# Streaming encoder step on one core: twelve conditioning pieces in the gating stage, and two pauses in each pair of columns of the column sums

## The chip, the core and the metric

The kernel runs on one core of a Trainium2 chip. The metric is the device time of one execution in microseconds. Before the change it is 2128.83 us, the median of three runs (2127.75 to 2129.07).

## What is computed

The reference is one step of a small encoder of two layers with d = 1024, for a prompt of 1024 rows and a sample of 32 rows, which share all weights but have conditioning vectors of their own:

```
mod = silu(c) @ w_ada[i] + b_ada[i]                 # 6 x 1024 per layer: sh1, sc1, gt1, sh2, sc2, gt2
h   = rmsnorm(x) * (1 + sc1) + sh1
mix = layer 0: gating mixer:  u, v = split(gelu(h @ w_in)); v = rmsnorm(v)
               mix = (u * (W_s v + b_s)) @ w_out    # W_s within chunks of 128 rows, 8 groups
      layer 1: pooling mixer: trailing means over 2, 4, 8, 16 rows, minus h, a matrix per group
x   = x + gt1 * rmsnorm(mix)
h   = rmsnorm(x) * (1 + sc2) + sh2
x   = x + gt2 * rmsnorm(relu(h @ w_up)^2 @ w_down)  # 1024 -> 4096 -> 1024
```

All arrays are float32. `w_ada` alone holds 2 x 1024 x 6144 numbers, which are used once, for two vectors.

## The kernel before, in words

**Tiles.** The 1056 rows are the columns of three tiles (`TILES`): tile 0 and tile 1 of 384 prompt columns, tile 2 of 256 prompt and 32 sample columns. Channels lie along the partitions. Every large product is made of three matmuls of float32r (high x high, high x low, low x high, `products` L952 to L963), so each weight is split into a high part (ScalarE, L441) and a low part (VectorE, by `tt`, whose line in the profile is L80).

**Stages.** (1) Run-in with a hand-written order. (2) The `v` half of the gating mixer's first product (`pv`). (3) The gating stage, from about 245 to 617 us: six entries of `mixes` (L372), each two groups and a list of tiles. Mixes 0 and 1 take all three tiles, mixes 2 and 3 tile 0 alone, mixes 4 and 5 tiles 1 and 2. `sgu_item` makes for each tile four `up` blocks (`pu`, 24 matmuls each), after each second one the gating product (`psp`) with `gate`, and leaves `down` (`po`, eight output blocks of twelve matmuls) pending: it is emitted after the first `up` block of the next tile (`flush`, L1534). (4) Layer 0's feed-forward network: `passes` of 512 hidden channels. Some passes take one tile; the six passes `COMBINED[0]` take tiles 0 and 1 together in a form with seven products in place of eight (`combined_item`, `pf_0a` to `pf_1c`, L1625), from about 756 to 1147 us. These need, beside the columns themselves, four sums and differences of columns of tiles 0 and 1, which `sums_of_columns` (L1808) makes ahead of the stage: `sum_columns` (L1839) once for each of four pairs of columns. (5) Tile 2's passes, woven with the pooling mixer; layer 1's passes; four paired passes (`COMBINED[1]`) from about 1655 to 1908 us; tile 2's last passes and the output.

**The weight stream.** All weights come through one list, `stream`, in the order in which they are used: gating weights by `w_groups`, feed-forward weights by `w_chunk`, and between them the conditioning pieces of `w_ada`, 512 KB each, by `some_ada` (L347), which appends the next n of the list `rest`. Loads are issued on SP's queue by `issue` (L409) into three buffers `raw` (L178) in the order of the stream. `stream_step` (L658) takes the next item: `do_w` splits a weight, `do_s` (L463) makes the seven weight combinations of a paired pass out of a load, and `do_ada` (L539) multiplies a conditioning piece by the conditioning values: four VectorE operations of 128 x 512 per piece into `aa`, and after every fourth piece two transposes, a reduction and, later, a small matmul (`ada`, L528).

**The order.** The source is a program that plans as it emits. `time["pe"]` and `time["dve"]` (L66) add up estimated times of TensorE and VectorE; `tick` keeps VectorE's at most 4 us behind. After each block `weave` (L758) takes at most one item of the stream (not a conditioning piece while VectorE's clock is more than 0.5 us ahead of TensorE's, `stream_waits` L695), then pulls `fillers` while VectorE's clock is behind. `need_w` (L704), called where a matmul needs a weight, takes items until that weight is there, whatever they are. A gating weight may be split when the weight eight places ahead of it has been used for the last time (L651). Fillers are generators: norms, residuals, the pooling mixer, the column sums. What a generator yields tells `pull` (L728) how to go on: `False` leaves it in its place, `True` puts it on `sticky`, so that it is the next to be pulled, and a number closes it until the planner's TensorE clock has passed the present by as many microseconds, while the next filler may go. `finish` pulls a filler to its end at once where its result is needed.

The instructions thus emitted are then put in an order for each engine by the framework, which schedules by readiness with the emission order as rank; on the chip each engine runs its list in that fixed order.

**Where the change touches.** In the loop over `mixes` (L374 to L377), in the loop over `passes` (L378 to L381), and in `sum_columns` (two `yield True`, L1855 and L1869). There, for each pair of columns, three loads from `md` are followed by four subtractions on VectorE, four roundings on ScalarE (L1866, L1868) and four low parts on VectorE.

Of the kernel before, what the change touches and what calls it, by code (L numbers as in the profile page):

```python
# [35 lines left out]
def tile_stream_encoder_step(  # L36
# [128 lines left out]
    def t_m(name):  # L165
        return work.tile([P, 384], F32, tag="m", bufs=3, name=name)
# [99 lines left out]
    def w_groups(n):  # L266
        gs, _ = mixes[n]
        for g in gs:
            for k in range(2):
                f = 2 * g + k  # L270
                add_w(
                    ("u", n, g, k),
                    sgu_w_in[0][:, f * P : (f + 1) * P].rearrange("(k p) f -> p k f", p=P),
                    (8, P),
                )
        for q in range(2):
            for g in gs:
                add_w(
                    ("o", n, g, q),
                    sgu_w_out[0][g * 256 : (g + 1) * 256, q * 512 : (q + 1) * 512].rearrange(  # L280
                        "(k p) d -> p k d", p=P
                    ),
                    (2, 512),
                )

    def w_chunk(n):
        l, c, _ = passes[n]
        if n in combined:
            for i in range(2):
                f0 = c * 512 + i * 256  # L290
                for q in range(2):
                    stream.append(
                        (
                            "s",
                            ("up", n, i, q),
                            ffn_w_up[l][q * 512 : (q + 1) * 512, f0 : f0 + 256].rearrange(
                                "(k p) f -> p k f", p=P
                            ),
                            (4, 256),
                        )  # L300
                    )
        for j in range(0 if n in combined else 4):
            f = 4 * c + j
            add_w(
                ("up", n, j),
                ffn_w_up[l][:, f * P : (f + 1) * P].rearrange("(k p) f -> p k f", p=P),
                (8, P),
            )
        for q in range(4):
            add_w(  # L310
                ("dn", n, q),
                ffn_w_down[l][c * 512 : (c + 1) * 512, q * 256 : (q + 1) * 256].rearrange(
                    "(j p) d -> p j d", p=P
                ),
                (4, 256),
            )
# [26 lines left out]
    combined = [n for r in runs for n in r]  # L343
# [3 lines left out]
    def some_ada(n):  # L347
        for _ in range(min(n, len(rest))):
            add, l, j = rest.pop(0)
            add(l, j)  # L350
# [22 lines left out]
    mixes += [((4, 5), every[1:]), ((6, 7), every[1:])]  # L373
    for n in range(len(mixes)):  # L374
        w_groups(n)
        if n < 2:
            some_ada(8)  # L377
    for n, (l, c, tiles) in enumerate(passes):  # L378
        w_chunk(n)
        if n in combined:  # L380
            some_ada(2 if l else 6 if n + 1 in combined else 2)  # L381
    assert not rest

    worder = [s[1] for s in stream if s[0] in "ws"]
# [70 lines left out]
    def temp(i):  # L455
        return scratch[:, 1024 + 384 * i : 1408 + 384 * i]
# [1351 lines left out]
    def sums_of_columns(l):  # L1808
        begun.add(l)
        n = ncol[0]  # L1810
        rooms = [room(part, NT - 1, f"sums_{part}", F32R) for part in "hl"]
        pieces = [
            r.rearrange("p k n -> p (k n)")[:, i * n : (i + 1) * n] for r in rooms for i in range(6)
        ]
        for name, tag, bufs, shape, k in (
            ("c", "c", 3, [P, 384], 1),
            ("r", "rr", 2, [P, 384], 1),
            ("w", "W", W_SLOTS, [P, 1024], 2),
        ):
            for i in range(w_taken[l] if tag == "W" else bufs):  # L1820
                x = work.tile(shape, F32R, tag=tag, bufs=bufs, name=f"sums_{name}{i}")
                pieces += [x[:, m * n : (m + 1) * n] for m in range(k)]
        for i in range(3):
            x = small.tile([P, 2, n], F32R, tag="x3", bufs=3, name=f"sums_x{i}")
            pieces += [x[:, 0], x[:, 1]]
        wide = late.tile([P, 2, 256], F32R, tag="wg", bufs=1, name="sums_g")
        pieces.append(wide.rearrange("p a b -> p (a b)")[:, :n])
        sums["spare"] = [pieces.pop(17) for _ in range(6)]
        sums["his"] = [pieces.pop(0) for _ in range(8)]
        sums["los"] = pieces  # L1830
        sums["parts"] = {}
        dsh = small.tile([P, 4], F32, tag="st", bufs=6, name="dshift")
        sh = shift[:, l, 1, :, 0].rearrange("p (k a) -> p k a", a=2)
        tt(out=dsh, in0=sh[:, :, 1], in1=sh[:, :, 0], op=ALU.subtract)
        sums["dsh"] = dsh
        for i in range(4):
            yield from sum_columns(l, i, (hh[0][:, 2 * i, :], hl[0][:, 2 * i, :]))

    def sum_columns(l, i, homes):  # L1839
        n = ncol[0]  # L1840
        dsh = sums["dsh"]
        home = {0: homes[0], 2: homes[1]}
        t1, t3, t2 = (temp(m) for m in range(3))
        t4 = t_m(f"sums_m{i}")
        nc.sync.dma_start(t1, md[1][:, 2 * i, :])
        nc.sync.dma_start(
            scratch[:, 1408:2176].rearrange("p (a n) -> p a n", a=2), md[0][:, 2 * i : 2 * i + 2, :]
        )
        nc.sync.dma_start(t4, md[1][:, 2 * i + 1, :])
        yield 3.0  # L1850
        tt(out=t1, in0=t3, in1=t1, op=ALU.subtract)
        tt(out=t3, in0=t2, in1=t3, op=ALU.subtract)
        tt(out=t2, in0=t2, in1=t1, op=ALU.subtract)
        tt(out=t4, in0=t4, in1=t2, op=ALU.subtract)
        yield True  # L1855
        todo = (
            (2, t3, dsh[:, i : i + 1]),
            (0, t1, None),
            (1, t2, shift[:, l, 1, 2 * i + 1, 0:1]),
            (3, t4, None),  # L1860
        )
        for j, src, b in todo:
            hi, lo = home[j] if j in home else sums["his"].pop(0), sums["los"].pop()
            sums["parts"][j, i] = hi, lo
            if b is None:
                act(out=hi, in_=src, func=AF.Copy)  # L1866
            else:
                act(out=hi, in_=src, func=AF.Identity, bias=b, scale=1.0)  # L1868
        yield True  # L1869
        for j, src, b in todo:  # L1870
            hi, lo = sums["parts"][j, i]
            if b is None:
                tt(out=lo, in0=src, in1=hi.bitcast(F32), op=ALU.subtract)
            else:
                stt(
                    out=lo,
                    in0=src,
                    scalar=b,
                    in1=hi.bitcast(F32),
                    op0=ALU.add,  # L1880
                    op1=ALU.subtract,
                )
        yield False
# [338 lines left out]
```

## Time and profile before

| | |
|---|---|
| median of the runs | 2128.83 us |
| profiled execution: its time, its span | 2128.48 us, 2126.7 us |
| VectorE busy, ScalarE busy | 74%, 49% of the span |
| DMA | 326.08 MB, 153 GB/s on average |
| VectorE busy in the gating stage (245 to 617 us) | 242.4 of 372 us |
| VectorE busy in the first paired stage (754 to 1147 us) | 317.6 of 393 us |
| VectorE busy in the second paired stage (1650 to 1908 us) | 165.5 of 258 us |
| conditioning pieces: loads, median time to landing | 96 of 512 KB, 4.6 us |

A span runs from the first to the last instruction. Busy times are unions of the instructions' times; matmuls overlap, so that one of 384 columns is listed with some 0.33 us while a new one begins about every 0.17 us. PE is TensorE, DVE VectorE, ACT ScalarE, SP the queue that issues the loads. In a line of the waits stand the waiting group, what released it, the time in all, the count and the longest. In a line of a timeline stand the start, the duration, engine, line, operation, out<-in, shape and count, and in brackets the idle time before it with its releaser. In a line of windows stand the stretch, its length, the busy time of PE, PEld, DVE, ACT and POOL, the granted clock of TensorE, the busy share of the DMA engines and GB/s. A line of the chain has start, duration and what ran, with the count.

### The profile page before, as it was taken

The numbers are of one execution on the slowest core, as the hardware profiler recorded it, in microseconds if no ns is written. First come the engines' busy times: TensorE is split into PE (matmuls) and PEld (weight loads), VectorE is DVE, ScalarE is ACT, GpSimd is POOL, SyncE is SP. The second block draws the span as 40 slices with busy tenths as digits, with TensorE's granted clock in tenths as the row PEclk, the third lists the DMA queues.
The fourth block names the chain that finished last, engine by engine and source line by source line (L and its number), as shares of the span: only waits on it lengthen the run. The fifth ranks groups of instructions, "written<-read, shape, count | busy, mean of one in ns | idle before, by whom it ended". The sixth has DMA issues, their size and how long they took to land.

```text
span 2126.7 us, 33204 instructions
## 1 busy us (share of the span) xinstructions
PE 2109.9 (99%) x12993; PEld 2035.4 (96%) x12993; DVE 1564.9 (74%) x2854; ACT 1032.6 (49%) x1808; POOL 15.3 (1%) x34
## 2 busy tenths in 40 slices
PE   9999999999999999999999999999999999999998
PEld 6878999999999999999999999999999999999998
DVE  6687747566879659987877987967768575588664
ACT  5534322234447554344446666665455453366454
POOL 0000000000000000000000000000000000000100
PEclk9999999999999999999999999999999999999999
DMA  8487524353537614343345675565356232258861
GB/s 309 140 278 211 168 85 131 93 150 104 174 94 241 190 52 148 121 137 111 116 156 175 197 246 164 154 197 166 108 155 194 70 106 78 62 172 254 205 184 38
DMA packets 368178, 326.08 MB, mean 153 GB/s; under 512 B 39858, under 2 KB 330202, under 8 KB 368020
## 3 DMA queue, kind: packets, MB, share of 16 engines
q1 hardware_dynamic: 367348, 323.06, 49.8%
q8 instruction: 102, 1.67, 0.3%
q0 software_dynamic: 640, 0.88, 0.1%
q14 instruction: 56, 0.46, 0.1%
q10 hardware_dynamic: 32, 0.01, 0.0%
HBM read 283.41 MB, written 40.49 MB: 152 GB/s over the span
## 4 chain that ended last, share of the span: by engine, by line
PE 88%; DVE 5%; DMA 4%; ACT 2%; issue 1%; SPq 0%; DVEq 0%; ACTq 0%
PE pg L961 10%; PE pg L963 10%; PE pg L962 10%; PE pf L961 6%; PE pf L962 5%; PE pf L963 5%; PE pf_0a L1625 4%; PE po L962 3%; PE po L961 3%; PE po L963 3%; PE pu L961 3%; PE pu L963 3%; PE pu L962 3%; PE pv L988 2%; PE pv L990 2%; PE pv L989 2%
## 5 line engine op out<-in xcount | busy, mean ns | idle before, releaser
L961 PE MATMUL pg<-fh,wh_dn 128*128 128x384 f32 (+1 forms) x1296 | 415.4, 321 | 2.7 <-ACT fh L1374 2.2
L963 PE MATMUL pg<-fh,wl_dn 128*128 128x384 f32 (+1 forms) x1296 | 412.2, 318 | 0.0
L962 PE MATMUL pg<-fl,wh_dn 128*128 128x384 f32 (+1 forms) x1296 | 412.1, 318 | 0.0
L961 PE MATMUL pf<-hh,wh_up 128*128 128x288 f32 (+1 forms) x896 | 281.0, 314 | 0.0
L962 PE MATMUL pf<-hl,wh_up 128*128 128x288 f32 (+1 forms) x896 | 279.2, 312 | 0.1
L963 PE MATMUL pf<-hh,wl_up 128*128 128x288 f32 (+1 forms) x896 | 278.8, 311 | 0.0
L961 PEld LDWEIGHTS pg<-fh,wh_dn 128*128 128x128 f32 x1296 | 243.1, 188 | 5.9 <-ACT fh L1374 3.6
L962 PEld LDWEIGHTS pg<-fl,wh_dn 128*128 128x128 f32 x1296 | 243.2, 188 | 0.7
L963 PEld LDWEIGHTS pg<-fh,wl_dn 128*128 128x128 f32 x1296 | 243.2, 188 | 0.7 <-DVE wl_dn L80 0.7
L80 DVE TENSOR_TENSOR acc<-acc,pg 128x384 f32<-128x384 f32 (+1 forms) x336 | 171.7, 515 | 64.6 <-PE pg L963 63.0
L80 DVE SCALAR_TENSOR_TENSOR aa<-raw,csil,aa 128x512 f32<-128x512 f32 (+1 forms) x364 | 204.9, 619 | 13.2 <-DMA raw<-in_w_ada_dram 13.2
L80 DVE TENSOR_TENSOR wl_dn<-raw,wh_dn 128x1024 fp32r<-128x1024 f32 x118 | 143.4, 1219 | 42.0 <-ACT wh_dn L441 41.0
L962 PEld LDWEIGHTS pf<-hl,wh_up 128*128 128x128 f32 x896 | 168.2, 188 | 0.9 <-DVE hl L80 0.3
L961 PEld LDWEIGHTS pf<-hh,wh_up 128*128 128x128 f32 x896 | 168.0, 188 | 0.9 <-ACT r L1549 0.2
L963 PEld LDWEIGHTS pf<-hh,wl_up 128*128 128x128 f32 x896 | 168.4, 188 | 0.0
L80 DVE TENSOR_TENSOR wl_up<-raw,wh_up 128x1024 fp32r<-128x1024 f32 (+2 forms) x141 | 128.2, 917 | 46.2 <-ACT wh_up L441 38.6
L441 ACT ACTIVATE wh_dn<-raw 128x1024 fp32r<-128x1024 f32 x118 | 124.1, 1055 | 75.3 <-PE pg L962 61.0
L441 ACT ACTIVATE wh_up<-raw 128x1024 fp32r<-128x1024 f32 x81 | 85.8, 1059 | 90.0 <-PE pf L962 56.9
L961 PE MATMUL pu<-hh,wh_u 128*128 128x384 f32 (+1 forms) x384 | 125.8, 328 | 0.0
L961 PE MATMUL po<-ush,wh_o 128*128 128x384 f32 (+1 forms) x384 | 123.5, 322 | 0.0
L963 PE MATMUL pu<-hh,wl_u 128*128 128x384 f32 (+1 forms) x384 | 123.4, 321 | 0.0
L962 PE MATMUL pu<-hl,wh_u 128*128 128x384 f32 (+1 forms) x384 | 123.4, 321 | 0.0
(456 smaller groups left out, 4556.0 us busy)
## 6 DMA issues: line engine op xcount, KB each, us to landing
raw<-in_ffn_w_up_dram SPq DMA_DIRECT2D x121, 512.0 KB, 4.1
raw<-in_ffn_w_down_dram SPq DMA_DIRECT2D x118, 512.0 KB, 3.5
raw<-in_w_ada_dram SPq DMA_DIRECT2D x96, 512.0 KB, 4.6
raw<-in_sgu_w_in_dram SPq DMA_DIRECT2D x40, 512.0 KB, 4.1
raws<-in_ffn_w_down_dram SPq DMA_DIRECT2D x30, 512.0 KB, 4.3
raws<-in_ffn_w_up_dram SPq DMA_DIRECT2D x27, 512.0 KB, 4.7
xd<-acc SPq DMA_DIRECT2D x8, 1536.0 KB, 7.4
raw<-in_sgu_w_out_dram SPq DMA_DIRECT2D x24, 512.0 KB, 3.7
```

The lines of the kernel that those rows point to most:

```text
L80: return op(out, *args, **kw)
L441: act(out=wh, in_=r, func=AF.Copy)
L961: mm(ps[:, :n], wh, rh, start=begin and i == 0, stop=False)
L962: mm(ps[:, :n], wh, rl, start=False, stop=False)
L963: mm(ps[:, :n], wl, rh, start=False, stop=end and i == last)
L988: mm(ps[:m, :], a_h, wh[:, o : o + 512], start=k == 0, stop=False)
L989: mm(ps[:m, :], a_h, wl[:, o : o + 512], start=False, stop=False)
L990: mm(ps[:m, :], a_l, wh[:, o : o + 512], start=False, stop=k == KB - 1)
L1625: mm(ps[:, :n], u, v, start=first and k == 0 and x == 0, stop=k == 3 and x == 2, skip_group_check=True,)
```

## The change

First, where conditioning pieces stand in the stream. Before, eight follow the gating weights of each of mixes 0 and 1; in the paired passes of layer 0 six follow each pass and two the last one, in those of layer 1 two each. After, eight, eight, eight and four follow mixes 0 to 3, five each (three for the last) the paired passes of layer 0, and none those of layer 1. So twelve more stand in the gating stage, four fewer in the first paired stage and eight fewer in the second; the order of the pieces among themselves is the same.

Second, `sum_columns` yields 1.5 in place of `True` after its subtractions and again after its roundings.

```
     for n in range(len(mixes)):
         w_groups(n)
-        if n < 2:
-            some_ada(8)
+        some_ada((8, 8, 8, 4, 0, 0)[n])
     for n, (l, c, tiles) in enumerate(passes):
         w_chunk(n)
         if n in combined:
-            some_ada(2 if l else 6 if n + 1 in combined else 2)
+            some_ada(0 if l else 5 if n + 1 in combined else 3)
...
         tt(out=t4, in0=t4, in1=t2, op=ALU.subtract)
-        yield True
+        yield 1.5
         todo = (
...
                 act(out=hi, in_=src, func=AF.Identity, bias=b, scale=1.0)
-        yield True
+        yield 1.5
         for j, src, b in todo:
```

More of the change, by code (lines that the diff above doesn't have):

```diff
@@ L375, in tile_stream_encoder_step @@
         w_groups(n)
-        if n < 2:
-            some_ada(8)
+        some_ada((8, 8, 8, 4, 0, 0)[n])
     for n, (l, c, tiles) in enumerate(passes):
@@ L1854, in sum_columns @@
         tt(out=t4, in0=t4, in1=t2, op=ALU.subtract)
-        yield True
+        yield 1.5
         todo = (
@@ L1868, in sum_columns @@
                 act(out=hi, in_=src, func=AF.Identity, bias=b, scale=1.0)
-        yield True
+        yield 1.5
         for j, src, b in todo:
```

2 lines of the change are left out of this document (1 added, 1 removed).

## The prediction

> **What bounds the kernel now.** I read the page first, then the waits of TensorE by stage, the table of windows, and last the timelines of VectorE, ScalarE and the DMA queue around the places that the change touches.
>
> ```profile
> PE 2109.9 (99%) x12993; PEld 2035.4 (96%) x12993; DVE 1564.9 (74%) x2854; ACT 1032.6 (49%) x1808; POOL 15.3 (1%) x34
> ```
>
> TensorE is the bound: 16.8 of 2126.7 us are idle. A change that leaves the matmuls alone can win only such idle time, and loses whatever new wait it gives TensorE. The waits, in the order gating stage (245 to 660 us), first paired feed-forward stage with the building of its sums (660 to 1130), second one (1560 to 1910):
>
> ```profile
> PE psp L1467 <- DMA vl<-vd: 0.7, 1, 0.7
> ```
> ```profile
> PE pg L961 <- ACT fh L1374: 1.4, 1, 1.4
> PE pf_1c L1625 <- DVE acc L80: 0.6, 1, 0.6
> PE pf_1a L1625 <- ACT acc L1642: 0.6, 1, 0.6
> ```
> ```profile
> PE pg L962 <- DVE sums_w L80: 1.5, 2, 0.8
> PE pg L961 <- ACT fh L1374: 0.8, 1, 0.8
> PE pf_1a L1625 <- ACT acc L1642: 0.6, 1, 0.6
> PE pg L961 <- DVE acc L80: 0.4, 1, 0.4
> PE pf_1c L1625 <- DVE acc L80: 0.2, 1, 0.2
> ```
>
> The stage that receives twelve pieces has no wait on VectorE today; the two that give them up have 6.1 us of waits together. A matmul of 384 columns shows 0.33 us but starts every 0.174 us (2.10 us for twelve, row below), so each wait also costs about 0.16 us of lost overlap: the nine of the last two fences are some 7.5 us in all, the most that could be won.
>
> **Gating stage: what comes in.** The weight stream is taken in order. `weave` (L758) takes at most one piece a call, eight calls per tile; an item of the stream that a matmul needs now makes `need_w` (L704) take all that stand before it at once. After the change eight conditioning pieces stand behind the weights of mix 2 and four behind those of mix 3. Mixes 2 and 3 have one tile each, 36 us. Of mix 2's eight calls two find nothing ready and four go to its own `o` weights (which follow those of mix 1 as these are released), so that two pieces are taken after its last two `up` blocks. The other six are forced by the first `up` of mix 3, which needs the `u` weight behind them, and they then rank ahead of that weight and of the accumulations of mix 2's `down`, emitted later (`flush`, L1534).
>
> When that weight is needed and when it is ready today:
>
> ```profile
> 447.99 0.42 PE L961 MATMUL pu<-hh,wh_u 128*128 128x384 f32 x1
> ```
> ```profile
> 433.36 1.22 DVE L80 TENSOR_TENSOR wl_o<-raw,wh_o 128x1024 fp32r<-128x1024 f32 x1
> 434.49 1.22 DVE L80 TENSOR_TENSOR wl_u<-raw,wh_u 128x1024 fp32r<-128x1024 f32 x1
> 437.82 0.62 DVE L80 SCALAR_TENSOR_TENSOR s<-psp,vec,bs 128x384 f32<-128x384 f32 x1 [2.11 <-PE psp L1467]
> ...
> 443.28 0.68 DVE L80 TENSOR_SCALAR wr<-wt,rv 128x128 f32<-128x128 f32 x3
> ...
> 447.60 0.62 DVE L80 SCALAR_TENSOR_TENSOR s<-psp,vec,bs 128x384 f32<-128x384 f32 x1 [2.51 <-PE psp L1467]
> ```
> ```profile
> 428.28 7.83 SPq L431 DMA_DIRECT2D raw<-in_sgu_w_in_dram  x4
> ```
>
> It is split at 434.5 to 435.7 and needed at 448.0: 12.3 us to spare. The four loads that start at 428.28 would be conditioning pieces. What such a piece costs, and how eight of them went in mix 1 of this kernel:
>
> ```profile
> 328.66 9.20 SPq L431 DMA_DIRECT2D raw<-in_w_ada_dram  x4
> ...
> 344.44 3.91 SPq L431 DMA_DIRECT2D raw<-in_w_ada_dram  x2
> ...
> 357.35 2.56 SPq L431 DMA_DIRECT2D raw<-in_w_ada_dram  x2
> ```
> ```profile
> 359.89 2.06 DVE L80 SCALAR_TENSOR_TENSOR aa<-raw,csil,aa 128x512 f32<-128x512 f32 x3
> ...
> 369.70 0.54 DVE L80 TENSOR_TENSOR acc<-acc,po 128x384 f32<-128x384 f32 x1
> 370.16 1.30 DVE L568 STREAM_TRANSPOSE raw<-aa 128x512 f32<-128x512 f32 x2
> 371.50 1.22 DVE L571 TENSOR_REDUCE sums<-raw 128x32 f32<-128x1024 f32 x1
> ```
>
> Three operations take 2.06 us, so a piece of four takes 2.7; every fourth piece adds transposes and a reduction, 2.5. Eight: 8 x 2.7 + 2 x 2.5 = 26.6 us of VectorE, with three raw buffers. By row the whole set of eight took from 328.7 to 372.7 in mix 1, 44 us, where nobody waited.
>
> The sum of VectorE's work. The first piece lands some 4 us after 428.3, at 432.3; until 448.0 that is 15.7 us. Ahead of the pieces stand one `wl_o` (1.2), the gating work from 437.82 to 443.96 less the `wl_u` in it (6.1 - 1.2 = 4.9), and the start of the second gating (0.6): 6.7. So 9.0 of 26.6 us are done by 448.0 and 17.6 remain; with the rest of the second gating (4.3, as in the first) and the weight itself (1.2) it is ready 23 us late, at 471. TensorE has cover: matmuls are put in an order other than the source's when operands are late (the next fence shows three products interleaved), so it can begin mix 2's `down`. There twelve matmuls take 2.1 us per output block, and three PSUM buffers (`ps_dn`, L159) hold three blocks, 6.3 us; the accumulations that free them rank behind the forced pieces. Two thirds of the first `up` block needs only `wh_u`, which needs no VectorE: another 2.8 us.
>
> ```profile
> 832.73 0.33 PE L1625 MATMUL pf_0b<-hl,wh_up 128*128 128x384 f32 x1
> 832.90 0.34 PE L1625 MATMUL pf_0c<-hl,sh_up 128*128 128x384 f32 x1
> 833.08 0.54 PE L1625 MATMUL pf_0a<-hh,wh_up 128*128 128x384 f32 x2
> ```
> ```profile
> 770.80 2.10 PE pf_0a L1625 x12
> ```
>
> That leaves 23 - 9.1 = 14 us of standstill. The other end: accumulations slip in between the pieces as at 369.70, all eight blocks (16.7 us) cover, and their 8 x 0.54 = 4.3 us are added: 23 + 4.3 - 16.7 - 2.8 = 8 us. The 44-us row gives, from 428.3, 472.3 plus 1.2 for the weight against 448.0 + 16.7: 8.8. I take **+9.5 us**, near that row, since those pieces had the same loads and gating work around them; 6 to 16 as bounds. The four pieces in mix 3 (10.8 + 2.5 = 13.3 us) are forced in the same way by mix 4's first `up`, but only four stand there, and 36 us hold them with the eight weights (9.8) and the gating work (11): 0, and up to 2 if not. On SP's queue a piece's load that waits for a raw buffer holds the `vl` loads of the next gating; the one such wait in the trace is 0.7 us, so 0, at most 1. The bytes (12 x 512 KB) are little in a stage that moves 123 GB/s. Fillers (tile 0's residual) are pulled only while the planner's VectorE clock is behind TensorE's, and by its rates (0.16 + 512/840 us an operation) twelve pieces add 12 x 3.1 us and more to it, so they start up to 40 us later; VectorE is busy 242 of 372 us of the stage, so they still end before the first feed-forward product needs them; 0, at most 2.
>
> ```profile
> 245.00:617.00 372.00, 371.26 (x2410) 369.93 (x2408) 242.40 (x473) 118.82 (x194) 2.50 (x8) 1.00 0.41 123
> ...
> 1908.00:2127.00 219.00, 211.30 (x1592) 210.68 (x1590) 145.61 (x218) 113.94 (x195) 9.95 (x16) 0.98 0.61 169
> ```
> ```profile
> 1.36 5.49 PE warm L1042 x12
> ...
> 41.37 16.77 PE pv L1203 x73
> ```
>
> A standstill of this length may also cost clock. The granted clock is 1.00 throughout and falls only in the last stage, where TensorE ends early; waits of up to 1.4 us lose nothing. After the start's idle time twelve matmuls of 512 columns took 5.49 us, against 12 x 0.23 = 2.8 later: 2.7 us lost. Between 0 and 2.7 I take **+1.5**. The Trainium skill ("TensorE: Matmul & The Clock Gate", Part 1, "What's actually happening") says that the clock halves after an idle window of about 3.4 us and comes back after a busy one. By it one to two windows at half rate would cost an estimated 1.7 to 3.4 us, and the sum would be 2135.7 to 2137.4; no run here shows such a gap yet.
>
> **What the paired stages give up.** In the second one all eight pieces go. Two rows before its waits at 1809 to 1815:
>
> ```profile
> 1805.32 2.73 DVE L80 SCALAR_TENSOR_TENSOR aa<-raw,csil,aa 128x512 f32<-128x512 f32 x4
> 1808.88 0.42 DVE L80 TENSOR_TENSOR acc<-raw 128x256 f32<-128x256 f32 x1 [0.82 <-DMA raw<-in_ffn_w_up_dram]
> ```
>
> The pieces hold VectorE and the raw buffer from which the next pass's weights come, and the splitting behind is late. Without them the waits on `sums_w` (1.5), on `acc` (0.4 and 0.2) should go: 2.1 us, with 0.16 for each of four waits **-2.7** (bounds -2.7 and 0: the splitting could still bunch). The first stage loses one piece of six per pass; its one wait on `acc` (0.6) and smaller ones: **-0.6** (bounds -1.0 and 0).
>
> **Column sums.** The subtracting, the rounding on ScalarE and the low parts are no longer pulled in one go; at each of two points other work may pass for 1.5 us. That may take away the waits on `fh` (1.4 and 0.8, with overlap 2.5 in two stages), which fall when sums and weight splitting crowd both engines. Against it the last column and a half instead of the last one is then forced at the start of the paired stage. It costs no more than a column's own work, about eight operations of 0.55 us: 4 us. **-0.7**, bounds -2.5 and +4.
>
> **Sum.** Profiled execution 2128.48 us (span 2126.7 and 1.8 around it; 0.35 below the median of 2128.83): +9.5 + 1.5 - 2.7 - 0.6 - 0.7 = +7.0, so **2135.5 us**. Its own range: 2130 to 2143.
>
> **Rivals.** *The pieces are hidden (faster).* Place: the first `up` of mix 3. If the order puts accumulations ahead of pieces, and the pieces begin earlier or cost less, `down` covers all. It decides at 16.7 + 2.8 us of VectorE's work left at 448.0, against my 27; five pieces in mix 2 rather than eight would fit. For it: VectorE idles 35% of the stage, and forced splitting at 830 is passed by interleaving without a wait. Then -2.7 - 0.6 - 0.7: 2124.5, or 2122.7 if the `fh` waits go whole. *The sums come too late (slower).* Late columns and forced residuals add up to 4 us in each paired stage on top of the standstill: 2140 to 2144. For it: the sums end at the start of the stage already. Against: the first summed product comes some 14 us into it. *No going round.* If `down` isn't moved ahead, TensorE stands the whole 23 us: 2128.5 + 23 + 1.5 - 4.0 = 2149; the interleaving at 830 us speaks against it. *The change does nothing:* weights are taken early enough and the waits stay, 2128.5.
>
> **Numbers.** This kernel can be told from no change at about 0.2%, 4.3 us: faster is below 2124.6, slower above 2133.1. Forecast 0.50 (0.44 slower, 0.06 within); hidden 0.33 (0.20 faster, 0.13 within); sums late 0.08, slower; no going round 0.04, slower; nothing 0.05, within. Together 0.20, 0.24 and 0.56. The range leaves out the 2149 and the extremes of the rest: 2122.5 to 2143.
>
> **What would show it.** Right: a gap of 6 to 16 us on TensorE around 454 us with VectorE full of `aa` rows, ended by `wh_u` or `wl_u`, with all matmuls behind it in TensorE's queue waiting too; clock under 1.00 after it; no `sums_w` wait in the second paired stage. Wrong: no wait over 2 us between 430 and 520 us, or `aa` rows that alternate with `acc` to the end of mix 2's `down`.

## The result, and the profile after

| kernel | time, median of 5 runs (range) | profiled execution / its span | ratio to before, 95% interval |
|---|---|---|---|
| before | 2128.83 us (2126.93 to 2131.02) | 2128.48 / 2126.7 us | |
| after | 2144.81 us (2142.23 to 2145.47) | 2144.81 / 2142.9 us | 1.0073, 1.006 to 1.0087 |

Of all executions behind the times in this document, two of e9_third_alone took 2528 and 7408 us; they are left out of its median and its ratio.

The change costs 16.0 us. The forecast had the sign and the place, but less than half of the size (+7.0, range to 2143.0). The first line of the page of the changed kernel, to be held against the first fence of the prediction:

```profile
PE 2114.2 (99%) x12993; PEld 2039.2 (95%) x12993; DVE 1562.8 (73%) x2854; ACT 1032.5 (48%) x1808; POOL 15.3 (1%) x34
```

The instructions are the same in number. Two things grew: TensorE's idle time, from 16.8 to 28.7 us, and its busy time, by 4.3 us, though it does the same work; that is a first sign of clock. TensorE's waits after, in the order gating stage, first paired stage, the single passes between the two paired stages (I call that stretch the middle), second paired stage:

```profile
PE pu L960 <- ACT wh_u L440: 9.8, 2, 8.4
PE psp L1466 <- DMA vl<-vd: 0.7, 1, 0.7
```
```profile
PE pg L960 <- DVE acc L80: 2.1, 1, 2.1
PE pg L960 <- ACT fh L1373: 0.7, 1, 0.7
...
```
```profile
PE pg L961 <- DVE fl L80: 1.1, 1, 1.1
PE pf L960 <- ACT r L1548: 0.7, 1, 0.7
```
```profile
PE pg L960 <- ACT fh L1373: 1.7, 1, 1.7
PE pf_1a L1624 <- ACT acc L1641: 0.6, 1, 0.6
...
```

In the names, `fh` and `fl` are the high and low parts of a block's hidden values and `r` is their squared relu before it is split; `acc` is the running sum into which finished blocks are added. The first line is the forecast standstill: 9.8 us in two pieces where there was nothing. The `acc` wait of 2.1 us and both lines of the third fence are new and were not forecast. The `sums_w` waits of the second paired stage are gone, as forecast.

A stage's length is counted from the first matmul of its first product to that of the next stage's, in the profiled execution:

| | gating and layer 0's single passes | first paired | middle | second paired | the end |
|---|---|---|---|---|---|
| before | 530.5 | 390.7 | 508.3 | 255.5 | 216.2 |
| after | 544.0 | 393.6 | 511.3 | 252.6 | 216.1 |
| difference | +13.4 | +2.9 | +3.0 | -2.9 | -0.1 |

**The place in the gating stage.** TensorE's timeline of the changed kernel: the last matmul of `down`'s third block, then the first `up` of mix 3, which starts twice:

```profile
454.44 0.34 PE L962 MATMUL po<-ush,wl_o 128*128 128x384 f32 x1
...
463.15 0.69 PE L960 MATMUL pu<-hh,wh_u 128*128 128x384 f32 x1 [8.37 <-ACT wh_u L440]
463.63 0.52 PE L961 MATMUL pu<-hl,wh_u 128*128 128x384 f32 x1
465.61 0.69 PE L960 MATMUL pu<-hh,wh_u 128*128 128x384 f32 x1 [1.46 <-ACT wh_u L440]
466.10 0.52 PE L961 MATMUL pu<-hl,wh_u 128*128 128x384 f32 x1
466.42 0.52 PE L962 MATMUL pu<-hh,wl_u 128*128 128x384 f32 x1
```

The wait is put down to `wh_u` on ScalarE. ScalarE had itself been idle for 11.43 us, waiting for the load; so the next view is SyncE's queue of loads, and beside it VectorE:

```profile
428.00 10.55 SPq L430 DMA_DIRECT2D raw<-in_w_ada_dram  x5
...
452.74 2.48 SPq L430 DMA_DIRECT2D raw<-in_w_ada_dram  x2
457.51 9.12 SPq L430 DMA_DIRECT2D raw<-in_sgu_w_in_dram  x4
```
```profile
453.42 9.36 DVE L80 SCALAR_TENSOR_TENSOR aa<-raw,csil,aa 128x512 f32<-128x512 f32 x14
462.69 1.30 DVE L567 STREAM_TRANSPOSE raw<-aa 128x512 f32<-128x512 f32 x2
463.91 1.19 DVE L80 TENSOR_TENSOR wl_u<-raw,wh_u 128x1024 fp32r<-128x1024 f32 x1
```

The four `u` loads that started at 428.28 before start at 457.51 now: eight pieces pass through three raw buffers first, and each buffer comes free only when VectorE is through with its piece. How full VectorE was, by stretch, after and then before (columns: stretch, its length, then the busy time of PE, PEld, DVE, ACT, POOL with the number of instructions, granted clock, DMA share, GB/s):

```profile
370.00:428.00 58.00, 58.00 (x396) 57.81 (x396) 30.54 (x69) 14.01 (x23) 0.31 (x1) 1.00 0.30 86
428.00:436.00 8.00, 8.00 (x57) 8.00 (x56) 6.58 (x11) 1.06 (x1) 0.00 (x0) 1.00 0.44 134
436.00:463.00 27.00, 18.73 (x115) 17.92 (x113) 26.90 (x49) 4.42 (x8) 0.00 (x0) 0.95 0.61 186
```
```profile
436.00:463.00 27.00, 27.00 (x167) 26.93 (x166) 16.81 (x32) 9.95 (x14) 0.00 (x0) 1.00 0.52 155
```

VectorE is busy 26.90 of 27.00 us there, after being idle for 27.5 of the 58 us before 428.

**The clock.** Twice after a standstill the granted clock is halved, here in stretches cut at its changes:

```profile
460.00:470.20 10.20, 5.59 (x16) 5.09 (x17) 9.75 (x19) 3.17 (x3) 0.00 (x0) 0.50 0.67 189
470.30:480.00 9.70, 9.70 (x57) 9.70 (x56) 5.92 (x7) 4.51 (x5) 0.00 (x0) 1.00 0.66 219
1139.30:1142.70 3.40, 1.32 (x8) 1.00 (x7) 3.40 (x12) 3.40 (x13) 0.00 (x0) 1.00 0.60 189
1142.80:1146.10 3.30, 3.30 (x12) 3.30 (x11) 2.94 (x8) 2.74 (x6) 0.00 (x0) 0.50 0.00 0
```

A matmul of 384 columns starts every 0.32 us there (466.10 and 466.42 above) instead of every 0.174. From 463.15, 16 matmuls take until 470.26: 7.11 us less the 1.46 of idle time is 5.65, against 2.8 at full clock, 2.9 us lost. With the idle 9.8 and some lost overlap that is the +13.4 of the stage. The second stretch costs 3.41 x (1 - 0.174 / 0.32) = 1.6 us.

**The end of the first paired stage.** VectorE of the changed kernel at the new `acc` wait:

```profile
1138.89 3.10 DVE L80 SCALAR_TENSOR_TENSOR hl<-acc,shift,hh 128x256 fp32r<-128x256 f32 x10 [1.16 <-ACT hh L1894]
1141.90 0.55 DVE L80 TENSOR_TENSOR acc<-acc,pg 128x384 f32<-128x384 f32 x1
```

Ten operations of tile 2's modulation (`late_modulation`) run in a row, and the accumulation that frees a PSUM buffer stands behind them: 2.1 us of waiting and 1.6 of half clock. In the kernel before, an accumulation comes after the first two of them and TensorE doesn't wait:

```profile
1124.86 0.65 DVE L80 SCALAR_TENSOR_TENSOR hl<-acc,shift,hh 128x256 fp32r<-128x256 f32 x2 [0.34 <-ACT hh L1895]
1125.43 0.55 DVE L80 TENSOR_TENSOR acc<-acc,pg 128x384 f32<-128x384 f32 x1
1125.89 1.20 DVE L80 SCALAR_TENSOR_TENSOR hl<-acc,shift,hh 128x256 fp32r<-128x256 f32 x4
```

Which part of the change puts them in one row is what the experiments had to find.

### The profile page after: what moved, and what is told of

The parts are those of the page before. It is cut to its first block, busy times and chain, and to the rows that moved or that the text cites. A ratio compares the mean times of both kernels' runs of the same rounds, so it can differ in the third digit from the quotient of the medians.

```text
span 2142.9 us, 33220 instructions
## 1 busy us (share of the span) xinstructions
PE 2114.2 (99%) x12993; PEld 2039.2 (95%) x12993; DVE 1562.8 (73%) x2854; ACT 1032.5 (48%) x1808; POOL 15.3 (1%) x34
## 4 chain that ended last, share of the span: by engine, by line
PE 89%; DVE 5%; DMA 3%; ACT 1%; issue 1%; SPq 0%; DVEq 0%; ACTq 0%
PE pg L960 11%; PE pg L962 11%; PE pg L961 11%; PE pf L960 5%; PE pf L961 5%; PE pf L962 5%; PE pf_0a L1624 4%; PE pf_1a L1624 4%; PE po L960 3%; PE po L961 3%; PE po L962 3%; PE pu L960 3%; PE pu L962 2%; PE pu L961 2%; PE pv L987 2%; PE pv L989 2%
## 5 line engine op out<-in xcount | busy, mean ns | idle before, releaser
L80 DVE TENSOR_TENSOR wl_up<-raw,wh_up 128x1024 fp32r<-128x1024 f32 (+1 forms) x142 | 129.2, 919 | 61.1 <-ACT wh_up L440 50.3
L961 PE MATMUL po<-usl,wh_o 128*128 128x384 f32 (+1 forms) x384 | 123.2, 321 | 0.0
```

Source lines behind the costliest of these rows:

```text
L80: return op(out, *args, **kw)
L961: mm(ps[:, :n], wh, rl, start=False, stop=False)
```

## The experiments

The theory after the result was: six pieces forced in a row at mix 3's first `up` cost the +13.4, and something in the paired stage the +5.9 behind it. For the second there were two candidates in the diff: the pauses in the building of the sums, and the new spread of the pieces over the passes (six and at last two became five and at last **three**). Every kernel was timed in five rounds, e7_no_load in three, beside runs of the kernel before on the same chip. The lists in brackets are pieces behind mixes 0 to 5, then pieces per pass of the first paired stage and in its last pass. The three columns on the right are of the one profiled execution; in e2_pauses, e3_spread, e10_burst_two, e12_early_one and e14_four_late it took 1.8 to 3.0 us more than the median. The ratios go by the runs of before on the same chip, so they, and not the medians, compare kernels timed on different chips.

| run | pieces | time, median | ratio, 95% interval | gating to the end of first paired | middle | second paired |
|---|---|---|---|---|---|---|
| before | [8 8 0 0 0 0] 6, 2; 2 in the second stage | 2128.83 | | 921.2 | 508.3 | 255.5 |
| after | [8 8 8 4 0 0] 5, 3 | 2144.81 | 1.0073 (1.006, 1.0087) | 937.6 | 511.3 | 252.6 |
| e1_pieces | as after, no pauses | 2142.48 | 1.0073 (1.006, 1.0085) | 936.6 | 510.2 | 252.5 |
| e2_pauses | as before, pauses | 2129.07 | 1.0006 (0.9997, 1.0015) | 921.2 | 511.5 | 254.6 |
| e3_spread | [8 8 4 0 4 4] 5, 3 | 2142.98 | 1.0074 (1.0062, 1.0087) | 937.2 | 511.2 | 254.1 |
| e4_reorder | as after, mix 3's u ahead | 2157.41 | 1.0143 (1.0129, 1.0156) | 950.9 | 510.9 | 252.0 |
| e5_early | [14 14 0 0 0 0] 5, 3 | 2130.82 | 1.0012 (1.0003, 1.0021) | 923.9 | 510.9 | 252.9 |
| e6_early_two | [15 14 0 0 0 0] 5, 2 | 2124.38 | 0.9982 (0.9973, 0.9991) | 921.1 | 507.7 | 252.2 |
| e7_no_load | as after, 8 without loads | 2131.0 | 1.0014 (1.0005, 1.0023) | 924.8 | 510.1 | 252.0 |
| e8_five | [11 12 5 0 0 0] 5, 3 | 2134.9 | 1.0029 (1.0018, 1.004) | 928.0 | 511.0 | 252.2 |
| e9_third_alone | [8 8 0 0 0 0] 6, then 5, 3; 2 | 2133.38 | 1.0027 (1.0016, 1.0038) | 924.1 | 511.2 | 255.8 |
| e10_burst_two | [8 8 8 5 0 0] 5, 2 | 2147.59 | 1.0096 (1.0082, 1.0109) | 945.8 | 507.9 | 252.1 |
| e11_early_two_no_pause | [15 14 0 0 0 0] 5, 2, no pauses | 2123.28 | 0.998 (0.9971, 0.9989) | 920.9 | 508.0 | 252.2 |
| e12_early_one | [16 14 0 0 0 0] 5, 1 | 2127.87 | 1.0 (0.9991, 1.0009) | 927.0 | 507.2 | 252.1 |
| e13_burst_odd_early | [9 8 8 4 0 0] 5, 2 | 2139.63 | 1.0056 (1.0043, 1.007) | 936.4 | 508.1 | 252.0 |
| e14_four_late | [13 12 0 4 0 0] 5, 2 | 2127.66 | 1.0 (0.9991, 1.0009) | 923.6 | 510.6 | 253.0 |

**Which half of the change.** e1_pieces takes the two pauses back:

```diff
-        yield 1.5
+        yield True
```

> The twelve moved pieces alone: the column sums are built without the two pauses, as before the change. Theory (burst): the six pieces that are forced ahead of mix 3's first u weight cost the whole +13.3 us of the gating stage (10.0 of standing still and some 3.3 at half clock); they are all here, so the gap at 454 us stays at 8 to 10 us and the second paired stage still wins 2.9. For the end of the first paired stage (2.1 us of waiting at 1140 us and 3.4 us of half clock) there are two explanations: if it comes from the third piece in the last pass, it stays, and the time is 2144 to 2146; if it comes from the pauses, it goes, and the time is 2139 to 2141.

e2_pauses has them alone, in the kernel before (the same two lines the other way round).

> The two pauses alone: the pieces stand where they stood before the change. Theory (burst): no gap in the gating stage, whose length is 530.6 us as before. If the pauses are what delays the end of the first paired stage, there is the wait on the accumulator at about 1140 us with its half clock, and the time is 2132 to 2135. If they are harmless, as the forecast has it (-0.7), it is 2126 to 2129.

The pieces alone cost as much as the whole change, the pauses alone nothing that can be told from zero. The wait at the end of the first paired stage is there without the pauses (3.1 us from 1139.9) and not there with the pauses alone. So it belongs to the pieces. A wait on `fh` where the second paired stage begins grew to 1.7 us in e2_pauses, with half clock behind it, which is its middle of 511.5; it lies between 0.3 and 1.7 us over the runs without a pattern that I found.

**Is it the row of eight, or the stage?** e3_spread keeps the number but puts four behind mix 2 and four each behind mixes 4 and 5:

```diff
-        some_ada((8, 8, 8, 4, 0, 0)[n])
+        some_ada((8, 8, 4, 0, 4, 4)[n])
```

> The same twelve pieces in the gating stage, but four behind the weights of mix 2, none behind mix 3's, four each behind mixes 4 and 5 (two tiles each, sixteen calls that can take a piece); the rest is the changed kernel. Theory (burst): four pieces, two of them taken before, leave at most two or three to be forced, which the down products cover: no gap over 1 us between 430 and 520 us, clock 1.00 there, 2144.8 - 13.3 = 2131.5, with 2129 to 2133 as bounds. Rival (the stage has no room for twelve pieces, whatever their order: VectorE or the three raw buffers): waits of 6 us or more appear elsewhere between 430 and 620 us, and the time is 2138 or more.

The gap at 454 us went, but the time stayed. The rival was right that something else comes in its place, though not for its reason. Waits of TensorE at the end of the gating stage:

```profile
PE pn_rs L852 <- ACT sc_rs L837: 4.1, 1, 4.1
PE pf L960 <- ACT hh L933: 1.8, 1, 1.8
...
```

Before, the first feed-forward product starts at 617.6 us, among the last `po` blocks, and hides the last tile's chain of norm and modulation. Here it starts at 639.0, behind the last `po`, so nothing is left to hide that chain, and the clock is halved for 10.24 us. The reason, read from the code and not tried by itself: tile 0's residual, which the first feed-forward product needs, is a filler that is pulled only while the planner's VectorE clock is behind, and the pieces behind mixes 4 and 5 keep that clock ahead. This is the term that the forecast put at "0, at most 2"; it holds in the changed kernel, but not for a later place.

**Is it the rank behind the pieces?** e4_reorder puts mix 3's `u` weights ahead of the eight pieces in the stream (`w_groups` gets the two switches `us` and `os` for it):

```diff
...
-        w_groups(n)
+        w_groups(n, us=n != 3)
+        if n == 2:
+            w_groups(3, os=False)
         some_ada((8, 8, 8, 4, 0, 0)[n])
```

> As many pieces as in the changed kernel behind mix 2 (eight), but mix 3's four u weights stand ahead of them in the stream, and only its o weights behind. Theory (rank: what costs is that the u weight stands behind the pieces): the first up of mix 3 finds its weight, the pieces have until mix 3's down, 36 us later: no gap at 454 us, 2131 to 2133. Rival (the amount: eight pieces in 36 us are too many for VectorE and the raw buffers): the standstill moves to the next product that needs a split weight or an accumulation, some 5 to 10 us at 460 to 500 us, and the time stays at 2139 to 2145.

The first `up` of mix 3 finds its weight, so the theory was right about the place. But the standstill comes whole one mix later, at 495 us, at mix 4's first `up`, and the late residual of e3_spread is added, which is why the time is above the rival's range as well:

```profile
PE pu L962 <- ACT wh_u L442: 9.5, 2, 8.0
PE pn_rs L854 <- ACT sc_rs L839: 3.8, 1, 3.8
PE pf L962 <- ACT hh L935: 1.8, 1, 1.8
```

The planner's order, worked through in the code, fits both kernels; the counts of calls in this paragraph come from the code and not from a trace. A mix of one tile has eight calls of `weave` and eight weights of its own to take. In the changed kernel two of mix 2's eight pieces get a call and six are forced; of mix 3's four, none gets one. Here five of the eight get a call, and the other three, mix 3's `o` weights and the next four pieces are all forced by mix 4's first `up`. What calls cannot take is put off to the next operation that cannot wait, not spread out. Mixes 0 and 1 have 24 calls each.

**Earlier.** e5_early therefore puts all twelve behind mixes 0 and 1.

```diff
-        some_ada((8, 8, 8, 4, 0, 0)[n])
+        some_ada((14, 14, 0, 0, 0, 0)[n])
```

> All twelve moved pieces earlier in the gating stage: fourteen behind the weights of mix 0, fourteen behind mix 1's (three tiles, 24 calls each; eight and eight before), none behind the later mixes. Theory (calls: a mix of one tile has eight calls and eight own weights, so every piece behind mixes 2 and 3 is left to be forced in a row; mixes 0 and 1 have calls to spare): no gap over 1 us in the gating stage, its length 530 to 532, the second paired stage keeps its gain of 2.9, the wait at 1139 us stays if the third piece in the last pass makes it: 2127 to 2131. Rival (no room in the stage, VectorE or loads): the forced row comes at the first up of mix 1 or of mix 2, or tile 0's residual is late at the end of the stage, 2135 or more.

The longest wait between 245 and 660 us is 0.5 us, and the stage is 530.8 long (530.5 before); the +13.4 are gone. What stays is the loss at the end of the first paired stage (2.8 us of waiting) and in the middle.

e6_early_two takes away that stage's third piece of the last pass as well (fifteen and fourteen, five and two).

```diff
-        some_ada((8, 8, 8, 4, 0, 0)[n])
+        some_ada((15, 14, 0, 0, 0, 0)[n])
...
-            some_ada(0 if l else 5 if n + 1 in combined else 3)
+            some_ada(0 if l else 5 if n + 1 in combined else 2)
```

> As the kernel with fourteen and fourteen, but fifteen behind mix 0 and two pieces rather than three in the last pass of the first paired stage. If the third piece makes the wait of 2 to 3 us on the accumulator at 1139 us, it is gone and the time is 2124 to 2128; if the wait has another cause (one piece less in each of the five passes before), it stays and the time is that of the kernel with fourteen and fourteen.

This beats both kernels. VectorE at the end of the first paired stage, to be held against the ten `hl` in a row above:

```profile
1124.75 0.65 DVE L80 SCALAR_TENSOR_TENSOR hl<-acc,shift,hh 128x256 fp32r<-128x256 f32 x2 [1.18 <-ACT hh L1894]
1125.32 0.55 DVE L80 TENSOR_TENSOR acc<-acc,pg 128x384 f32<-128x384 f32 x1
1125.78 2.32 DVE L80 SCALAR_TENSOR_TENSOR hl<-acc,shift,hh 128x256 fp32r<-128x256 f32 x8
1128.02 0.55 DVE L80 TENSOR_TENSOR acc<-acc,pg 128x384 f32<-128x384 f32 x1
```

An accumulation gets in between, and no wait on `acc` is left there. The middle is shorter too, 507.7 against 510.9: a wait on `fl` at 1271 to 1298 us and one on `r` at 1377 to 1404 us are in every run with a third piece, and at neither place is there a wait on them in a run with one or two. What the third piece does first can be seen on the queue of loads: in e5_early its own load starts at 1107.50 us and that of the next pass's first weight at 1110.57, while in e6_early_two the latter starts at 1107.81. How this later start puts the ten `hl` in one row, and why waits follow some 140 and 250 us behind it, is not shown.

e11_early_two_no_pause is e6_early_two with `yield True` for both `yield 1.5`.

> Fifteen and fourteen pieces behind mixes 0 and 1, two in the last pass, and the column sums built without pauses, as before the change. If the pauses do nothing, as their run alone says (1.0006, from 0.9997 to 1.0015), it is within 1.5 us of the kernel with pauses: 2123 to 2126. If the pauses help there, 2126 to 2129; if they cost, 2120 to 2123.

0.9980 against 0.9982, with intervals that overlap almost whole: the pauses do nothing here either. These two are the best kernels of the case.

e9_third_alone makes the reverse test in the kernel before, with 5 and 3 in the last two passes for 6 and 2.

```diff
-            some_ada(2 if l else 6 if n + 1 in combined else 2)
+            some_ada(2 if l else 3 if n + 1 not in combined else 6 if n + 2 in combined else 5)
```

> The kernel before the change with one edit: the fifth and the last pass of the first paired stage take 5 and 3 pieces, where they took 6 and 2; nothing else moves. Theory (the third piece of the last pass makes the loss at the end of that stage and behind it): a wait of 2 to 3 us on the accumulator about 15 us before the stage's end, small waits in the 510 us behind it, 2131 to 2135. Rival (the loss comes from having five pieces a pass, or from the state in which the gating stage leaves the queue): no such wait, 2127 to 2130.

```profile
PE pg L962 <- DVE fl L80: 1.5, 1, 1.5
PE pg L961 <- DVE acc L80: 1.5, 2, 1.1
PE pf L961 <- ACT r L1549: 0.7, 1, 0.7
```

One piece moved from the fifth pass to the sixth, and nothing else, brings the same three waits and costs 0.27% (0.16 to 0.38), 5.7 us by the ratio. VectorE's ten `hl` stand in one row there too, for 3.04 us from 1127.32.

**What is late: VectorE or the loads?** In e7_no_load the eight pieces behind mix 2 work on a constant; the reduction after each four of them is made in two halves, the rest of VectorE's work is the same:

```diff
...
+            if k in dry:
+                raws[k] = None
+                state["issued"] += 1
+                continue
...
```

> The changed kernel with the loads of mix 2's eight pieces left out: VectorE does the same operations on a constant (so these eight pieces' sums are not the reference's), and they take none of the three raw buffers. Theory (VectorE's time is what stands ahead of the u weight): wh_u is early, TensorE has a block or two of its products to do, but the low part wl_u still stands behind the pieces: a gap of 3 to 6 us near 454 us that VectorE ends, 2138 to 2142. Rival (raw buffers: the pieces hold them, so the u weight's load starts late, which is what the row of wh_u in the changed kernel says): the gap shrinks to under 1 us, 2130 to 2133.

The theory of VectorE's time fell: the stage is 531.3 long and its longest wait 0.8. But the run says more than that buffers matter. Without loads VectorE did these pieces in the idle time ahead of 428 us:

```profile
L80 DVE SCALAR_TENSOR_TENSOR aa<-raw,csil,aa x40: 744/749/756, 335.4 to 479.6; 128x512 f32<-128x512 f32 x40
L80 DVE SCALAR_TENSOR_TENSOR aa<-ident,csil,aa x28: 722/750/764, 372.5 to 405.7; 128x512 f32<-128x512 f32 x28
```

So VectorE had the time, some 40 us earlier. What kept the pieces out of it is their place in the stream: the weights of mix 2 stand ahead and, by the timeline of the queue, the pieces' loads start only at 428.0. From there VectorE's work and the buffers hold each other up, and no run here parts them.

e8_five tests the threshold that the forecast gave for a row that `down` still covers, five.

```diff
-        some_ada((8, 8, 8, 4, 0, 0)[n])
+        some_ada((11, 12, 5, 0, 0, 0)[n])
```

> Eleven pieces behind mix 0, twelve behind mix 1, five behind mix 2, none later; the paired stages as in the changed kernel. The forecast put the point from which down no longer covers the pieces at five behind mix 2. Theory (calls and cover): no standstill over 2 us at 454 us, 2127 to 2132. Rival (any forced row stops TensorE): a gap of 4 us or more there and half clock after it, 2134 or more.

The standstill shrinks to 1.9 us in two pieces, with no half clock, and the stage is 3.3 us longer than before; with four behind mix 2 (e3_spread) there was none, so the edge lies at about five. The theory was right about the standstill and missed the time by 2.9 us, since it left out the third piece, whose waits are all here (2.8 on `acc`, 1.5 on `fl`, 0.7 on `r`); the rival's time came without its gap.

e12_early_one goes on to one piece in the last pass.

```diff
-        some_ada((8, 8, 8, 4, 0, 0)[n])
+        some_ada((16, 14, 0, 0, 0, 0)[n])
...
-            some_ada(0 if l else 5 if n + 1 in combined else 3)
+            some_ada(0 if l else 5 if n + 1 in combined else 1)
```

> Sixteen and fourteen pieces behind mixes 0 and 1, one piece in the last pass instead of two or three. Theory (the end of the paired stage decides, and with two pieces nothing waits there any more): the same as with two, 2123 to 2126. Rival (each piece less in the last pass saves its own work): another 2 to 5 us less, 2119 to 2122. If fourteen and sixteen are too many for mixes 0 and 1, a gap appears before 440 us.

Neither was right: it is 0.18% slower than with two, some 3.8 us. The middle stays short (507.2), but there are waits on `sums_w` near 1118 us and one of 1.9 us on `fh` at 752 with half clock. Why that is so is open; two is the best of the three counts, not the start of a trend.

**How the two losses add.** e10_burst_two keeps the row and puts the third piece behind mix 3.

```diff
-        some_ada((8, 8, 8, 4, 0, 0)[n])
+        some_ada((8, 8, 8, 5, 0, 0)[n])
...
-            some_ada(0 if l else 5 if n + 1 in combined else 3)
+            some_ada(0 if l else 5 if n + 1 in combined else 2)
```

> The changed kernel with the third piece of the last pass put behind mix 3 instead (eight, eight, eight, five, none, none, and five and two in the first paired stage). Theory (two separate losses: the forced row at mix 3's first up, and the third piece): the gap of 8 to 10 us at 454 us stays with its half clock, the wait at 1140 us goes: 2137 to 2141, some 5 to 6 us below the changed kernel. Rival (the wait at 1140 us follows from the burst): 2143 to 2146.

The wait at the end of the paired stage went, and the middle is 507.9, as the theory had it; the time was missed, since a fifth piece behind mix 3 made a second standstill (1.9 us on `wl_u` at 506 us) and two more stretches of half clock. e13_burst_odd_early puts that piece behind mix 0 instead:

```diff
-        some_ada((8, 8, 8, 4, 0, 0)[n])
+        some_ada((9, 8, 8, 4, 0, 0)[n])
...
-            some_ada(0 if l else 5 if n + 1 in combined else 3)
+            some_ada(0 if l else 5 if n + 1 in combined else 2)
```

> The changed kernel with one edit: the third piece of the last pass goes behind mix 0 (nine, eight, eight, four, none, none, and five and two in the first paired stage), so the row forced at mix 3's first up is as in the changed kernel. Theory (two losses that add: the forced row with its half clock, +13 in the gating stage; the third piece, +5 to +6 behind it): the gap of 8 to 10 us at 454 us stays, no wait over 1 us at the end of the first paired stage, 2137.5 to 2140. Rival (the loss behind the gating stage follows from its delay): 2143 to 2146.

Its waits in the gating stage, then in the first paired stage:

```profile
PE pu L960 <- ACT wh_u L440: 9.0, 2, 8.6
PE pu L962 <- DVE wl_u L80: 1.3, 1, 1.3
```
```profile
PE pg L960 <- ACT fh L1373: 1.0, 1, 1.0
PE pf_1c L1624 <- DVE acc L80: 0.6, 2, 0.3
```

The row is untouched, the `acc` wait of 2.1 us is gone, and the time falls by 5.2 us between the medians, by 3.6 by the ratios, whose intervals overlap. Together with e5_early and e6_early_two, which were timed side by side and lie 6.4 us apart, this closes the account within that scatter: two losses that add, about 13 us for the row and about 4 to 6 for one piece in the wrong pass.

e14_four_late runs the four pieces behind mix 3 without the eight behind mix 2.

```diff
-        some_ada((8, 8, 8, 4, 0, 0)[n])
+        some_ada((13, 12, 0, 4, 0, 0)[n])
...
-            some_ada(0 if l else 5 if n + 1 in combined else 3)
+            some_ada(0 if l else 5 if n + 1 in combined else 2)
```

> Thirteen and twelve pieces behind mixes 0 and 1, none behind mix 2, four behind mix 3, two in the last pass. Theory (the forecast's term for these four: nothing, at most 2 us, since 36 us of VectorE hold them): within 2 us of the kernel with fifteen and fourteen, 2123 to 2126. Rival (a mix of one tile has no call for a piece, so even four are forced in a row at mix 4's first up, and tile 0's residual comes late behind them): a gap of 1 to 3 us at about 505 us with half clock, 2127 to 2132.

```profile
PE psp L1466 <- DVE wr L80: 0.9, 1, 0.9
PE po L960 <- ACT ush L1373: 0.7, 1, 0.7
```

Neither was right: the time lies in the rival's range without the rival's gap. There is none at 505 us, but there are two small waits, a stage of 533.8 (+3.1 on e6_early_two) and, this time, the `fh` wait with half clock before the second paired stage. By these rows the four cost 1.6 us and the overlap around them when they stand alone.

## Why the prediction was right in kind and wrong in size

| term | forecast | measured in the changed kernel |
|---|---|---|
| standstill at mix 3's first `up` | +9.5 (6 to 16) | +9.8 |
| clock behind it | +1.5 (0 to 2.7) | +2.9 |
| first paired stage, and the middle, which had no term | -0.6 | +5.9 |
| second paired stage | -2.7 | -2.9 |
| column sums | -0.7 | not to be told from 0 (e2_pauses) |
| sum | +7.0 | +16.1, with 0.7 of lost overlap and small waits in the gating stage and -0.3 outside (16.2 between the two profiled spans, 16.0 between the medians) |

**The standstill** came at the forecast place, after three blocks of `down`, and with the forecast length, but the length was in part luck. The value was taken near the 44-us row, and both sides of that estimate were too long: the pieces' last multiply ended at 462.8 us and `wl_u` was ready at 465.1, where the row gave 473.5, and `down` covered 6.3 us, where it gave 16.7. Inside the sum of VectorE's work, too, two errors cancelled. By 448 us, 16 of the pieces' 32 multiply operations were done, where I had a third. And the 2.8 us of cover by products that need only `wh_u` never came, since its load was as late as VectorE: `wh_u` began at 462.0 and `wl_u` at 463.9.

**The clock term** was mis-sized. I set it between nothing and the 2.7 us of the start and took the middle; it was 2.9. The forecast's own remark that waits of up to 1.4 us lose nothing was true and was stretched too far: 2.1 us at 1140 cost a halved stretch as well. The Trainium skill ("TensorE: Matmul & The Clock Gate", Part 1, "What's actually happening") gives half clock after an idle window of about 3.4 us, in windows that run on freely; the estimate of 1.7 to 3.4 us that the prediction drew from it holds 2.9, though not by its working: three steps of 3.41 us were halved, not one or two, and TensorE stood idle for 4.5 of those 10.24 us. Its idle window does not hold here: less than a whole one sufficed, as the last section shows.

**The step that failed** is "the first stage loses one piece of six per pass". The diff takes five for six in the first five passes but three for two in the last, and the forecast costed the average. The modulation of tile 2 falls on the last pass and shares VectorE with the accumulations of that pass; that is where a piece more costs. e9_third_alone prices it at 5.7 us by itself, e5_early against e6_early_two at 6.4, and e13_burst_odd_early at 3.6 to 5.2 within the changed kernel; half of it falls in the middle, for which the forecast had no term. Of the 9 us by which the forecast was short, 6.5 lie there.

**The second paired stage** gave what its waits promised, -2.9 for -2.7. **The column sums** gave nothing; the `fh` waits that they were to relieve went on changing from run to run.

**The rivals.** That the pieces are hidden was refuted; its threshold of five was about right: e8_five left 1.9 us of standstill, where eight pieces left 9.8. That the sums come too late did not occur, though its range (2140 to 2144) came nearest to the time: the end of the paired stage did lose, by another hand. "No going round" was refuted by three blocks of `po`.

## What to carry to other kernels

When work is moved in an ordered stream, count who has a turn to take it: places with as many calls as own weights have none, and what is put there is taken in one row by the next operation that cannot wait. Idle time of an engine is only of use where the work's loads can start before it, so move such work ahead of the loads that would block its buffers, not behind them. And read a changed schedule pass by pass: an average that falls can hide a last pass that rises, and the last pass is where other work begins; the moved pieces were worth 0.2% (0.9982, 0.9973 to 0.9991) in the right places (thirteen in e6_early_two) and cost 0.7% in the wrong ones (twelve).

## What the runs showed of the hardware that was not expected

The halved clock comes in steps. Away from the start and the end, every halved stretch in these sixteen kernels lasts 3.41, 6.83, 10.24 or 13.65 us, multiples of one step, and each begins a whole number of steps after the first rise to full clock, which comes between 4.3 and 7.5 us into the profile. What counts at full clock is how much of one step stood idle, not how long the gap was. The same gap of 2.8 us at the same place, in e8_five and then in e5_early, in rows cut at the steps of each:

```profile
1130.30:1133.70 3.40, 0.62 (x4) 0.44 (x3) 3.40 (x12) 3.40 (x12) 0.00 (x0) 1.00 0.49 158
1133.70:1137.10 3.40, 3.40 (x13) 3.40 (x12) 2.80 (x7) 2.60 (x6) 0.00 (x0) 0.50 0.00 0
```
```profile
1125.60:1129.00 3.40, 1.98 (x12) 1.66 (x10) 2.23 (x7) 2.77 (x9) 0.00 (x0) 1.00 0.99 296
1129.00:1132.40 3.40, 2.02 (x11) 2.02 (x12) 3.40 (x11) 3.40 (x10) 0.00 (x0) 1.00 0.16 56
1132.40:1135.80 3.40, 3.40 (x22) 3.40 (x21) 3.40 (x10) 2.08 (x5) 0.00 (x0) 1.00 0.00 0
```

In e8_five the gap lies within one step, and the next one runs at half clock, which costs an estimated 1.6 us, as worked out above. In e5_early it is split, 1.4 us in each of two steps, and costs nothing more. In the changed kernel 2.08 us idle in one step were enough. Over the sixteen kernels, every step at full clock with 2.0 us or more of idle time was followed by a halved one, and none with 1.65 or less was; between 1.84 and 1.91 both occurred. Once the clock is halved, far less keeps it so: 1.46 us idle in the halved step from 463.51 us of the changed kernel, and 0.41 in that from 638.56 of e3_spread, were followed by another halved step, 0.28 in that from 465.64 of e1_pieces was not. At the very end listed idle time is not the measure: before, the step from 2116.53 us has 0.65 us of it and the next is halved, but twelve of its matmuls have two columns. So the Trainium skill ("TensorE: Matmul & The Clock Gate", Part 1, "What's actually happening") is borne out in the length of the step and in its running on freely, and not in that a whole step has to be idle. Since the steps lie otherwise in each execution, part of the spread of 2 to 5 us between executions of one kernel may come from them; that was not tested.
